# Two of three gate projections by Strassen's scheme on every second pair of weight rows, and a merge that goes branch by branch

## The chip, the cores and the metric

The kernel runs on one core of a Trainium2 chip. The metric is the device time of one execution in microseconds (us), the median of several runs. A profiled execution of the same kernel gives the trace from which all rows below come.

## The reference, cut to what matters

One decoder layer over 256 tokens of 2048 channels: a combined input projection, three token mixers, a gated merge, an output projection and a layer norm, all in float32.

```python
u = x @ w_in[l]                                   # 256 x 2048 by 2048 x 16896
(a_q, ..., c_g, m_a, m_b, m_c) = jnp.split(u, split_idx, axis=-1)
y_a = (o_a * silu(a_g)) @ w_proj_hgrn[l]          # 256 x 1024 by 1024 x 2048
y_b = (o_b * silu(b_g)) @ w_proj_attn[l]
y_c = (o_c * silu(c_g)) @ w_proj_conv[l]
merged = sigmoid(m_a) * y_a + sigmoid(m_b) * y_b + sigmoid(m_c) * y_c
x = layer_norm(ALPHA * x + merged @ w_out[l], ln_g[l], ln_b[l])
```

The change concerns `m_b` and `m_c`, the gate projections of the second and third branch: each is a product of 256 x 2048 by 2048 x 2048.

## The kernel before

A float32 product is made of three matmuls in a rounded format (float32r). Each operand is split into a part `hi` (the value rounded) and a part `lo` (the rest), and hi*hi + lo*hi + hi*lo is accumulated in PSUM. `x` is split once, into the tiles `xs`. The weights are split as they stream in: `load_granule` issues a DMA of 1 MB into one of three buffers `raw` (on SP's queue), and `split_w` makes of each half of it `hi` (a cast on ACT, L111) and `lo` (a subtraction on DVE, L112). `hi` and `lo` have four buffers each, of 128 x 1024.

`gemm` accumulates one block of 512 output columns for both halves of the tokens in two of the four PSUM banks `acc`. In the form "rows" (L140 to L142) one half granule serves two k-tiles (128 rows of weights each), two token halves and three matmuls, so 12 matmuls of 128x512.

The merge is the loop over four blocks `d` of 512 columns, and in it over the three branches: the gate (`rows512`, 16 k-tiles), its sigmoid (L637, on ACT), the projection of the branch (8 k-tiles), and on DVE the product with the gate and the sum (L641, L642, L644). `turn` transposes a finished block `merged` on TensorE (tiles `mT`, L259) and splits it into a tile `m`, the stationary operand of the output projection `w_out`. It is a task: `pump` lets it take one step after each half granule.

Around that stage: the conv mixer (`conv`, four calls) ends the mixers, and splits its result `yc` into the tiles `outs["c"]` (`oc`). In the merge all of this goes through a scheduler, which sets the order of instructions on each engine when the kernel is built; each engine then works through its own list in that order.

Of the kernel before, what the change touches and what calls it, by code (L numbers as in the profile page):

```python
# [36 lines left out]
HALF = 1024  # L37
# [11 lines left out]
def hybrid_kernel(ctx, tc, a, out):  # L49
    nc = tc.nc  # L50
# [22 lines left out]
    def bank(name):  # L73
        return bgp.tile([P, NC], F32, tag="bg", name=name)

    def f32(ap):
        return ap.bitcast(F32)


    xs = [t8([P, 4, 2, T], f"xs{i}", F32R) for i in range(4)]  # L80

    def split_to(dst, src):

        nc.scalar.copy(out=dst[:, :, 0], in_=src)
        nc.vector.tensor_sub(out=dst[:, :, 1], in0=src, in1=f32(dst[:, :, 0]))
# [7 lines left out]
    tasks = []  # L93
# [41 lines left out]
    def accumulators():  # L135
        return [accp.tile([P, NC], F32, tag="acc", name="acc") for _ in range(2)]
# [419 lines left out]
    ps = bank("warm")  # L556
# [4 lines left out]
    for hf in range(2):  # L561
        v = rows_out(rows512(AI + hf, None if hf else first), "va")
        q = t4([P, 4, T], "qa")
        for u in range(2):
            acc = columns256(AQ + 2 * hf + u)
# [7 lines left out]
        for u in range(2):  # L573
# [15 lines left out]
    acc = columns256(BK)  # L589
# [9 lines left out]
    for hf in range(2):  # L599
        gate = t4([P, 4, T], "gb")  # L600
        for u in range(2):
            acc = columns256(BG + 2 * hf + u)
# [5 lines left out]
        for u in range(2):  # L608
            acc = columns256(BQ + 2 * hf + u)
# [20 lines left out]
    branches = ((MA, "w_proj_hgrn", "a"), (MB, "w_proj_attn", "b"), (MC, "w_proj_conv", "c"))  # L630
    for d in range(4):
        m = t4([P, 2, NC], "merged")
        for n, (mc, wp, br) in enumerate(branches):
            acc = rows512(mc + d)
            sg = t4([P, 2, NC], "sg")
            for t in range(2):
                nc.scalar.activation(out=sg[:, t], in_=acc[t], func=AF.Sigmoid)  # L637
            acc = gemm(a[wp][d], outs[br], NC, "rows")
            for t in range(2):
                if n:  # L640
                    nc.vector.tensor_mul(out=sg[:, t], in0=acc[t], in1=sg[:, t])  # L641
                    nc.vector.tensor_add(out=m[:, t], in0=m[:, t], in1=sg[:, t])  # L642
                else:
                    nc.vector.tensor_mul(out=m[:, t], in0=acc[t], in1=sg[:, t])  # L644
        tasks.append(turn(m))
# [41 lines left out]
    for n in range(3):  # L687
        acc = gemm(a["w_out"][n], ms, NC, "rows")
# [3 lines left out]
    for g in range(4):  # L692
        raw = load_granule(a["w_out"][3, g])
# [18 lines left out]
def _weights(w, n):  # L712

    k, m = w.shape
    per = 2 * HALF // n
    return np.ascontiguousarray(
        w.reshape(k // (P * per), per, P, m // n, n).transpose(3, 0, 2, 1, 4)
    ).reshape(m // n, k // (P * per), P, 2 * HALF)


def _w_in(w):

    segment = lambda at, width: w[:, at : at + width]
# [75 lines left out]
```

## Time and profile before

| what | value |
|---|---|
| median of 3 runs | 1021.34 us (1020.45 to 1021.34) |
| the profiled execution | 1020.65 us, of it 1018.9 us span from the first to the last instruction |
| busy share of the span | TensorE 99%, its weight loads 83%, DVE 65%, ACT 51%, GpSimd 3% |
| granted TensorE clock | 0.996 of full speed |

The span is the stretch of the trace, and the time of the execution has 1.75 us more. A matmul's end is modelled and matmuls overlap, so the busy share says only that TensorE was hardly ever without one; its pace is read from the distance between starts.

### The profile page before, as it was taken

Reading aid. Unit: us, or ns where it says so; the run is one execution under the profiler, and the core shown is the slowest. Engines: PE = TensorE matmul, PEld = TensorE weight load, DVE = VectorE, ACT = ScalarE, POOL = GpSimd, SP = SyncE. Lnnn points to the kernel's source line nnn. Section 1 sums busy time; section 2 is a strip of 40 time slices with the busy share of each in tenths; the row PEclk is TensorE's granted clock in tenths of the full one; section 3 lists DMA queues with packets and bytes.
Section 4 is the critical chain, followed back from the end, with each engine's and each line's share of the span. In section 5 each row is a group of like instructions: output and inputs, shape, how many; then the busy total and the mean of one; then the engine's idle time right before and its main releaser. Section 6 shows DMA issues by size and latency. Waiting matters only on the chain.

```text
span 1018.9 us, 13636 instructions
## 1 busy us (share of the span) xinstructions
PE 1004.3 (99%) x5502; PEld 848.5 (83%) x5502; DVE 659.5 (65%) x828; ACT 516.9 (51%) x702; POOL 32.4 (3%) x32
## 2 busy tenths in 40 slices
PE   8999999999999999999999999999999999999995
PEld 5888888888888888888888888888888888888885
DVE  6557789689965777777764455445545455546666
ACT  5546577656564655656554434444444434444341
POOL 1000000300010000000000000000000000000003
PEclk9999999999999999999999999999999999999998
DMA  8654535353565445444455555555555546765442
GB/s 326 243 197 175 206 130 202 130 204 125 186 210 183 166 168 205 165 166 165 166 180 192 207 186 186 203 177 197 191 184 203 196 176 248 252 243 200 171 166 83
DMA packets 30255, 192.63 MB, mean 189 GB/s; under 512 B 3776, under 2 KB 4576, under 8 KB 8176
## 3 DMA queue, kind: packets, MB, share of 16 engines
q1 hardware_dynamic: 28368, 184.85, 51.1%
q10 hardware_dynamic: 1152, 4.72, 1.3%
q0 software_dynamic: 672, 2.20, 0.7%
q8 instruction: 43, 0.70, 0.3%
q14 instruction: 20, 0.16, 0.0%
HBM read 189.63 MB, written 2.12 MB: 188 GB/s over the span
## 4 chain that ended last, share of the span: by engine, by line
PE 94%; DVE 4%; DMA 1%; issue 0%; SPq 0%; ACT 0%
PE acc L148 23%; PE acc L142 19%; PE acc L140 19%; PE acc L141 19%; PE acc L147 11%; DVE lo L112 1%; PE sc L461 1%; DMA raw<-in_w_rows 1%; PE pvb L504 1%; PE acc L150 1%; PE pT L494 1%; PE pv L413 0%; PE mT L259 0%; PE lev L375 0%; PE lev L387 0%
## 5 line engine op out<-in xcount | busy, mean ns | idle before, releaser
L112 DVE TENSOR_TENSOR lo<-raw,hi 128x1024 fp32r<-128x1024 f32 (+1 forms) x341 | 414.9, 1220 | 289.4 <-ACT hi L111 288.3
L111 ACT CAST hi<-raw 128x1024 fp32r<-128x1024 f32 (+1 forms) x341 | 356.7, 1048 | 384.9 <-PE acc L141 264.4
L148 PE MATMUL acc<-xs,hi 128*128 128x512 f32 x1056 | 371.9, 396 | 0.0
L147 PE MATMUL acc<-xs,lo 128*128 128x256 f32 x990 | 278.5, 281 | 0.0
L148 PEld LDWEIGHTS acc<-xs,hi 128*128 128x128 f32 x1056 | 197.0, 188 | 43.7
L140 PE MATMUL acc<-hi,xs 128*128 128x512 f32 (+1 forms) x544 | 210.6, 387 | 1.3 <-ACT hi L111 1.3
L142 PE MATMUL acc<-lo,xs 128*128 128x512 f32 (+1 forms) x544 | 208.6, 384 | 0.8 <-DVE lo L112 0.8
L141 PE MATMUL acc<-hi,xs 128*128 128x512 f32 (+1 forms) x544 | 208.6, 383 | 0.0
L147 PEld LDWEIGHTS acc<-xs,lo 128*128 128x128 f32 x990 | 186.8, 189 | 2.3
L140 PEld LDWEIGHTS acc<-hi,xs 128*128 128x128 f32 x544 | 102.5, 188 | 23.9 <-ACT hi L111 3.8
L142 PEld LDWEIGHTS acc<-lo,xs 128*128 128x128 f32 x544 | 102.1, 188 | 22.4 <-DVE lo L112 2.3
L141 PEld LDWEIGHTS acc<-hi,xs 128*128 128x128 f32 x544 | 102.6, 189 | 19.6
L188 ACT COPY rest<-acc 128x256 f32<-128x256 f32 x66 | 24.3, 373 | 43.6 <-PE acc L148 42.8
L140 PE MATMUL acc<-hi,m 128*128 128x512 f32 (+1 forms) x120 | 45.2, 376 | 0.0
L142 PE MATMUL acc<-lo,m 128*128 128x512 f32 (+1 forms) x120 | 45.0, 375 | 0.0
L141 PE MATMUL acc<-hi,m 128*128 128x512 f32 (+1 forms) x120 | 45.0, 375 | 0.0
L141 PEld LDWEIGHTS acc<-hi,m 128*128 128x128 f32 x120 | 22.6, 188 | 4.0
L140 PEld LDWEIGHTS acc<-hi,m 128*128 128x128 f32 x120 | 22.6, 188 | 4.0
L142 PEld LDWEIGHTS acc<-lo,m 128*128 128x128 f32 x120 | 22.6, 188 | 4.0
L140 PE MATMUL acc<-hi,oa 128*128 128x512 f32 x64 | 24.9, 389 | 0.0
L141 PE MATMUL acc<-hi,oa 128*128 128x512 f32 x64 | 24.9, 389 | 0.0
L142 PE MATMUL acc<-lo,oa 128*128 128x512 f32 x64 | 24.9, 389 | 0.0
(187 smaller groups left out, 900.3 us busy)
## 6 DMA issues: line engine op xcount, KB each, us to landing
raw<-in_w_cols SPq DMA_DIRECT2D x68, 1024.0 KB, 4.8
raw<-in_w_rows SPq DMA_DIRECT2D x60, 1024.0 KB, 4.8
raw<-in_w_out SPq DMA_DIRECT2D x16, 1024.0 KB, 4.8
raw<-in_w_proj_hgrn SPq DMA_DIRECT2D x8, 1024.0 KB, 4.7
raw<-in_w_proj_attn SPq DMA_DIRECT2D x8, 1024.0 KB, 4.8
raw<-in_w_proj_conv SPq DMA_DIRECT2D x8, 1024.0 KB, 4.8
raw<-in_w_rows SPq DMA_DIRECT2D x7, 512.0 KB, 8.4
bias<-bias_dr POOLq DMA_DIRECT2D x2, 1024.0 KB, 6.1
```

The costliest lines, as they stand in the source:

```text
L111: nc.scalar.copy(out=hi, in_=r)
L112: nc.vector.tensor_sub(out=lo, in0=r, in1=f32(hi))
L140: nc.tensor.matmul(out=acc, lhsT=xk[:, 0, ts], rhs=hi, start=first, stop=False)
L141: nc.tensor.matmul(out=acc, lhsT=xk[:, 1, ts], rhs=hi, start=False, stop=False)
L142: nc.tensor.matmul(out=acc, lhsT=xk[:, 0, ts], rhs=lo, start=False, stop=last)
L147: nc.tensor.matmul(out=acc[:, :T], lhsT=lo, rhs=xk[:, 0], start=False, stop=False)
L148: nc.tensor.matmul(out=acc, lhsT=hi, rhs=xk, start=first, stop=last)
L150: nc.tensor.matmul(out=acc[:, :T], lhsT=lo, rhs=xk[:, 0], start=False, stop=False)
L188: nc.scalar.copy(out=rest[p], in_=acc[p, T:])
L461: nc.tensor.matmul(out=ps[:, o_ : o_ + 2 * nk], lhsT=q[:, 2 * g + x, m, blk * P : blk * P + P], rhs=kz[n][:, hf, :, 0:nk], start=(i == 0), ...
L494: nc.tensor.transpose(out=ps[:, x * P : x * P + P], in_=s[:, x // 2, x % 2, j * P : j * P + P], identity=C["ident"])
L504: nc.tensor.matmul(out=ps, lhsT=v[m][:, j, c], rhs=pT[n][:, j], start=(j == 0 and i == 0), stop=(j == blk and i == 2))
```

## The change

The gates of branches b and c are computed by `gate_pair`, one call for two blocks of 512 columns. The weights come in a layout of their own (`w_gate`): a granule of 1 MB holds a pair of k-tiles by 1024 columns, as four pieces of 128 x 512. A call goes through eight such pairs. Pairs 0, 2, 4 and 6 are done as before: 2 k-tiles by 2 column blocks by 2 token halves, 8 products of three matmuls each. Pairs 1, 3, 5 and 7 are done by a scheme of Strassen's kind with 7 products instead of 8. Its sums of weights are made on DVE (`w`, three instructions over 2048 columns in all) and split into `hw` (ACT) and `lw` (DVE); its sums of `x` are made once (`sums_of_x`). All products of a call accumulate in eight PSUM banks (`p1` to `p7` and `px`), four of them from the pool `bg` that the transposes use too. At the end one copy on ACT and eight sums on DVE make the two gates of the eight banks, and two sigmoids follow.

The merge goes branch by branch: branch a for all four blocks, then for b and for c two calls of `gate_pair`, each followed by the two projections of its blocks. The four blocks `merged` live through all of it. `oc` is split after the third call of `gate_pair` instead of in `conv`. The blocks are transposed in the last two projections and in `w_out`.

```diff
+PAIRS = (0, 1, 0, 1, 0, 1, 0, 1)
...
-        nc.vector.tensor_mul(out=y, in0=y, in1=h)
-        if u % 2 == 0:
-            outs["c"].append(t8([P, 4, 2, T], "oc", F32R))
-        split_to(outs["c"][-1][:, 2 * (u % 2) : 2 * (u % 2) + 2], y)
+        nc.vector.tensor_mul(out=yc[:, 2 * u : 2 * u + 2], in0=y, in1=h)
...
+    def sums_of_x():
+        n = len(pairs)
+        xr = rawp.tile([P, n, 2, T], F32, tag="raw", name="xr")
...
+        nc.vector.tensor_add(out=sx[:, 0], in0=x21, in1=x22)
+        nc.vector.tensor_sub(out=sx[:, 1], in0=sx[:, 0], in1=x11)
+        nc.vector.tensor_sub(out=sx[:, 2], in0=x21, in1=x11)
+        nc.vector.tensor_sub(out=sx[:, 3], in0=x12, in1=sx[:, 1])
+        yield
+        for i in range(0, n, 2):
+            dst = t8([P, 2, 4, 2, P], "sums", F32R)
+            sums.append(dst)
+            for j in range(2):
+                split_to(dst[:, j].rearrange("p s h t -> p s h t"), sx[:, :, i + j])
+            yield
...
+            w = t8([P, 4, NC], "w")
+            nc.vector.tensor_sub(out=w[:, 0:2], in0=raw[:, 0:1].to_broadcast([P, 2, NC]), in1=raw[:, 1::2])
+            nc.vector.tensor_sub(out=w[:, 2], in0=raw[:, 3], in1=w[:, 0])
+            nc.vector.tensor_sub(out=w[:, 3], in0=raw[:, 2], in1=w[:, 2])
+            hi, lo = split_w(flat[:, NC : 3 * NC])
...
+            split_w(flat[:, 3 * NC :], hi2, lo2)
...
+            split_w(w, hw, lw)
...
+            product(p1, block(k, 0), hi[:, :NC], lo[:, :NC], end)
+            product(p2, block(k + 1, 0), hi[:, NC:], lo[:, NC:], end)
+            pump()
+            product(p6, sx[1], hw[:, 2], lw[:, 2], end)
+            product(p7, sx[2], hw[:, 1], lw[:, 1], end)
+            product(p5, sx[0], hw[:, 0], lw[:, 0], end)
+            product(p3, sx[3], hi2, lo2, end)
+            product(p4, block(k + 1, 1), hw[:, 3], lw[:, 3], end)
+            pump()
...
+        nc.scalar.copy(out=one, in_=p1)
+        nc.vector.tensor_add(out=sg[0][:, 0], in0=p2, in1=one)
...
+        for y in sg:
+            nc.scalar.activation(out=y, in_=y, func=AF.Sigmoid)
...
+    for n, (wp, br) in enumerate((("w_proj_attn", "b"), ("w_proj_conv", "c"))):
+        for half in range(2):
+            sg = gate_pair(a["w_gate"][2 * n + half])
...
+            if br == "c" and half:
+                tasks.extend(turn(merged[d]) for d in range(2))
+            for j in range(2):
+                d = 2 * half + j
+                acc = gemm(a[wp][d], outs[br], NC, "rows")
...
+                if br == "c" and half:
+                    tasks.append(turn(merged[d]))
```

What the scheduler makes of it is shown at three places, as rows of an engine's list (line, operation, output <- inputs, size, and how often in a row).

First, DVE inside the merge. Before, in a block `d`:

```order
L112 TENSOR_TENSOR lo<-raw,hi 128x1024 x12
L641 TENSOR_TENSOR sg<-acc,sg 128x512 x2
L642 TENSOR_TENSOR merged<-merged,sg 128x512 x2
L112 TENSOR_TENSOR lo<-raw,hi 128x1024 x3
L85 TENSOR_TENSOR m<-mT,m 128x2x256
L112 TENSOR_TENSOR lo<-raw,hi 128x1024
L85 TENSOR_TENSOR m<-mT,m 128x2x256
```

Now, inside the second call of `gate_pair`, with buffer numbers; raw_6572 holds a direct pair, raw_6533 and raw_6606 the Strassen pairs before and behind it:

```order
L115 TENSOR_TENSOR lw_6548<-w_6535,hw_6547 128x2048
L115 TENSOR_TENSOR lo_6575<-raw_6572,hi_6574 128x1024
L691 TENSOR_TENSOR w_6608<-raw_6606 128x1024
L115 TENSOR_TENSOR lo_6591<-raw_6572,hi_6590 128x1024
L692 TENSOR_TENSOR w_6608<-raw_6606,w_6608 128x512
L115 TENSOR_TENSOR lo_6613<-raw_6606,hi_6612 128x1024
L693 TENSOR_TENSOR w_6608<-raw_6606,w_6608 128x512
L115 TENSOR_TENSOR lo_6617<-raw_6606,hi_6616 128x512
L115 TENSOR_TENSOR lw_6621<-w_6608,hw_6620 128x2048
```

Where one kind of instruction stood in long runs, DVE's list now repeats a group of eight for every two pairs, and `lw` stands two places behind the last sum `w` of its own pair.

Second, DVE at the end of the same call, where raw_6735 and those behind it hold the next projection:

```order
L115 TENSOR_TENSOR lo_6690<-raw_6679,hi_6689 128x512
L115 TENSOR_TENSOR lo_6738<-raw_6735,hi_6737 128x1024
L115 TENSOR_TENSOR lo_6754<-raw_6735,hi_6753 128x1024
L722 TENSOR_TENSOR sg_6718<-p2_6419,one_6721 128x512
L723 TENSOR_TENSOR u_6720<-p6_6420,one_6721 128x512
L115 TENSOR_TENSOR lo_6772<-raw_6769,hi_6771 128x1024
L724 TENSOR_TENSOR sg_6718<-p7_6421,u_6720 128x512
L725 TENSOR_TENSOR sg_6719<-p5_6422,u_6720 128x512
L726 TENSOR_TENSOR sg_6719<-p5_6422,sg_6718 128x512
L728 TENSOR_TENSOR sg_6719<-p3_6423,sg_6719 128x512
L727 TENSOR_TENSOR sg_6719<-p8_6425,sg_6719 128x512
L729 TENSOR_TENSOR sg_6718<-p4_6424,sg_6718 128x512
```

Three of the four halves of the projection's first block are split ahead of the last six sums. Before, the gates took nothing from DVE here (the first piece above).

Third, ACT around the start of `w_out`. Before, the last projection's sigmoids, then the first casts of `w_out` with the transposed last block `m` among them:

```order
L637 ACTIVATE sg<-acc 128x512
L111 CAST hi<-raw 128x1024
L637 ACTIVATE sg<-acc 128x512
L111 CAST hi<-raw 128x1024 x6
L84 CAST m<-mT 128x2x256
L111 CAST hi<-raw 128x1024
L84 CAST m<-mT 128x2x256
L111 CAST hi<-raw 128x1024 x16
```

Now, from the cast of the last half of the last projection on:

```order
L114 CAST hi<-raw 128x1024
L87 CAST m<-mT 128x2x256
L114 CAST hi<-raw 128x1024
L87 CAST m<-mT 128x2x256
L767 DMA xres_7858<-in_x 128x2048
L87 CAST m<-mT 128x2x256
L767 DMA xres_7859<-in_x 128x2048
L769 DMA lg<-in_ln_g 128x2048
L770 DMA lbt<-in_ln_b 128x2048
L87 CAST m<-mT 128x2x256
L114 CAST hi<-raw 128x1024
L87 CAST m<-mT 128x2x256
```

Only one half of `w_out` is cast ahead of the last block's two casts `m`, and the second half stands between them. On TensorE the eight transposes of that block follow directly behind the first 12 matmuls of `w_out`:

```order
L145 MATMUL acc<-lo,m 128x512
L262 MATMUL mT<-ident,merged 128x128 x8
L143 MATMUL acc<-hi,m 128x512
L144 MATMUL acc<-hi,m 128x512
L143 MATMUL acc<-hi,m 128x512
L144 MATMUL acc<-hi,m 128x512
L145 MATMUL acc<-lo,m 128x512 x2
```

Before, they came in two groups of four, behind the first 24 and the first 36 matmuls of `w_out`.

## Rows read from the trace of the kernel before

**Rows 1.** The page: busy time of the engines, and the chain that ended last.
```profile
PE 1004.3 (99%) x5502; PEld 848.5 (83%) x5502; DVE 659.5 (65%) x828; ACT 516.9 (51%) x702; POOL 32.4 (3%) x32
...
PE 94%; DVE 4%; DMA 1%; issue 0%; SPq 0%; ACT 0%
```

**Rows 2.** Stages: last mixers, whole merge, one block of it.
```profile
core 0: us, PE busy (x) PEld busy (x) DVE busy (x) ACT busy (x) POOL busy (x), PEclk, DMA share, GB/s
513.00:925.00 412.00, 412.00 (x1848) 341.66 (x1846) 216.19 (x204) 176.95 (x188) 0.00 (x0) 1.00 0.57 202
628.00:727.00 99.00, 99.00 (x443) 82.00 (x442) 51.52 (x48) 41.98 (x45) 0.00 (x0) 1.00 0.54 192
400.00:513.00 113.00, 112.98 (x646) 98.07 (x645) 85.41 (x130) 65.21 (x112) 0.00 (x0) 1.00 0.47 165
```

**Rows 3.** Waits in the merge: engine, line, waited for, us, times, longest.
```profile
ACT hi L111 <- PE acc L141: 213.8, 133, 2.2
DVE lo L112 <- ACT hi L111: 190.5, 138, 2.0
```

**Rows 4.** TensorE in order of time in a gate of the merge: start, us.
```profile
540.21 0.39 PE L140 MATMUL acc<-hi,xs 128*128 128x512 f32 x1
...
541.57 0.39 PE L140 MATMUL acc<-hi,xs 128*128 128x512 f32 x1
```

**Rows 5.** DVE in order of time where it never idled, in the mixers.
```profile
229.81 0.70 DVE L352 TENSOR_TENSOR PS<-PS 128x512 f32<-128x512 f32 x1
230.42 0.70 DVE L361 TENSOR_TENSOR e<-qc,el 128x512 f32<-128x512 f32 x1
231.02 0.70 DVE L353 TENSOR_TENSOR PS<-PS 128x512 f32<-128x512 f32 x1
231.62 1.23 DVE L112 TENSOR_TENSOR lo<-raw,hi 128x1024 fp32r<-128x1024 f32 x1
232.76 0.70 DVE L307 TENSOR_TENSOR nl<-e,nh 128x512 fp32r<-128x512 f32 x1
```

**Rows 6.** ACT in order of time where a gate ends.
```profile
545.85 0.60 ACT L637 ACTIVATE sg<-acc 128x512 f32<-128x512 f32 x1 [1.21 <-PE acc L142]
546.34 1.04 ACT L111 CAST hi<-raw 128x1024 fp32r<-128x1024 f32 x1
547.28 0.60 ACT L637 ACTIVATE sg<-acc 128x512 f32<-128x512 f32 x1
```

**Rows 7.** DVE in order of time behind a projection.
```profile
918.69 1.37 DVE L641 TENSOR_TENSOR sg<-acc,sg 128x512 f32<-128x512 f32 x2
919.97 1.29 DVE L642 TENSOR_TENSOR merged<-merged,sg 128x512 f32<-128x512 f32 x2
921.17 1.22 DVE L112 TENSOR_TENSOR lo<-raw,hi 128x1024 fp32r<-128x1024 f32 x1
```

**Rows 8.** DMA issues: median us from issue to landing, of 1 MB.
```profile
raw<-in_w_rows SPq DMA_DIRECT2D x60, 1024.0 KB, 4.8
```

**Rows 9.** The chain near the conv mixer's first call, in order of time.
```profile
249.26 0.60 DVE oc L85
...
251.69 1.24 DVE lo L112
252.97 0.38 PE acc L142
```

**Rows 10.** TensorE there: the wait in brackets.
```profile
252.97 0.38 PE L142 MATMUL acc<-lo,xs 128*128 128x256 f32 x1 [0.46 <-DVE lo L112]
```

**Rows 11.** TensorE at the start of `w_out`.
```profile
924.61 0.60 PE L259 MATMUL mT<-ident,merged 128*128 128x128 f32 x4
924.97 0.48 PE L140 MATMUL acc<-hi,m 128*128 128x512 f32 x1
```

**Rows 12.** ACT there.
```profile
924.58 1.05 ACT L111 CAST hi<-raw 128x1024 fp32r<-128x1024 f32 x1 [1.67 <-PE acc L141]
925.53 0.58 ACT L84 CAST m<-mT 128x512 fp32r<-128x512 f32 x1
```

More of the change, by code (lines that the diff above doesn't have):

```diff
@@ L40 @@
 POOL = 512
-AI, AG, MA, MB, MC = 0, 2, 4, 8, 12
+AI, AG, MA = 0, 2, 4
+PAIRS = (0, 1, 0, 1, 0, 1, 0, 1)
 AQ, AFG, BQ, BG, BK, BV = 0, 4, 8, 12, 16, 17
@@ L57, in hybrid_kernel @@
     w8 = ctx.enter_context(tc.tile_pool(name="w8", bufs=12))
-    w4 = ctx.enter_context(tc.tile_pool(name="w4", bufs=7))
     sm = ctx.enter_context(tc.tile_pool(name="sm", bufs=4))
+    mixers = ctx.enter_context(ExitStack())
+    w4 = mixers.enter_context(tc.tile_pool(name="w4", bufs=7))
     drp = ctx.enter_context(tc.tile_pool(name="drp", bufs=1, space=bass.MemoryType.DRAM))
@@ L579, in hybrid_kernel @@
         tasks.append(hgrn(hf, fk, q, v, gate))
+    yc = t8([P, 8, T], "yc")
     conv(0)
@@ L617, in hybrid_kernel @@
     pump(100)
+    mixers.close()
+    mgp = ctx.enter_context(tc.tile_pool(name="mgp", bufs=1, reuse_waits="tile"))
     ms = []
@@ L624, in turn @@
         ms.append(dst)
-        yield
         for i, ps in transpose_pairs([[m[:, t, c * P : c * P + P] for t in range(2)] for c in range(4)], "mT"):
@@ L628, in turn @@
             yield
-    branches = ((MA, "w_proj_hgrn", "a"), (MB, "w_proj_attn", "b"), (MC, "w_proj_conv", "c"))
-    for d in range(4):
[L632 to L645, printed above, removed]
+    pairs = [p for p in range(KT // 2) if PAIRS[p]]
@@ new lines, in hybrid_kernel @@
+    sums = []
+    def sums_of_x():
+        n = len(pairs)
+        xr = rawp.tile([P, n, 2, T], F32, tag="raw", name="xr")
+        for i, p in enumerate(pairs):
+            nc.sync.dma_start(out=xr[:, i], in_=a["xT"][:, 2 * p : 2 * p + 2])
+        x11, x21 = xr[:, :, 0, :P], xr[:, :, 0, P:]
+        x12, x22 = xr[:, :, 1, :P], xr[:, :, 1, P:]
+        sx = t8([P, 4, n, P], "sx")
+        nc.vector.tensor_add(out=sx[:, 0], in0=x21, in1=x22)
[9 more added lines that the diff above has]
+            yield
@@ new lines, in gate_pair, with product, block @@
+    def gate_pair(src):
+        p1, p2, p6, p7 = [accp.tile([P, NC], F32, tag="acc", name=f"p{i}") for i in (1, 2, 6, 7)]
+        p5, p3, p4, px = [bgp.tile([P, NC], F32, tag="bg", name=f"p{i}") for i in (5, 3, 4, 8)]
+        begun = set()
+        def product(ps, x, hi, lo, last):
+            begins = id(ps) not in begun
+            begun.add(id(ps))
+            nc.tensor.matmul(out=ps, lhsT=x[0], rhs=hi, start=begins, stop=False)
+            nc.tensor.matmul(out=ps, lhsT=x[1], rhs=hi, start=False, stop=False)
+            nc.tensor.matmul(out=ps, lhsT=x[0], rhs=lo, start=False, stop=last)
+        def block(k, t):
+            return [xs[k // 4][:, k % 4, i, t * P : t * P + P] for i in range(2)]
+        last = KT // 2 - 1
+        final = max(p for p in range(KT // 2) if not PAIRS[p])
+        for p in range(KT // 2):
+            raw = rawp.tile([P, 4, NC], F32, tag="raw", name="raw")
+            nc.sync.dma_start(out=raw, in_=src[p].rearrange("p (s n) -> p s n", s=4))
+            flat = raw.rearrange("p s n -> p (s n)")
+            if not PAIRS[p]:
+                for s in range(2):
+                    hi, lo = split_w(flat[:, s * HALF : s * HALF + HALF])
+                    k = 2 * p + s
+                    for c in (slice(0, NC), slice(NC, HALF)):
+                        second = (c.start == 0) == (s == 0)
+                        for t in (1, 0):
+                            ps = ((p2, p3), (p4, px))[t][second]
+                            product(ps, block(k, t), hi[:, c], lo[:, c], p == final and s == 1 and ps is px)
+                    pump()
+                continue
+            w = t8([P, 4, NC], "w")
[3 more added lines that the diff above has]
+            hi, lo = split_w(flat[:, NC : 3 * NC])
+            hi2 = hip.tile([P, HALF], F32R, tag="hi", name="hi")[:, :NC]
+            lo2 = lop.tile([P, HALF], F32R, tag="lo", name="lo")[:, :NC]
+            split_w(flat[:, 3 * NC :], hi2, lo2)
+            if pairs.index(p) % 2:
+                hw, lw = t8([P, 4, NC], "hw", F32R), t8([P, 4, NC], "lw", F32R)
+            else:
+                hw = mgp.tile([P, 4, NC], F32R, tag="hw", name="hw")
+                lw = mgp.tile([P, 4, NC], F32R, tag="lw", name="lw")
+            split_w(w, hw, lw)
+            i = pairs.index(p)
+            sx = [sums[i // 2][:, i % 2, j] for j in range(4)]
+            sx = [[y[:, 0], y[:, 1]] for y in sx]
+            k = 2 * p
+            end = p == last
+            product(p1, block(k, 0), hi[:, :NC], lo[:, :NC], end)
[6 more added lines that the diff above has]
+            product(p4, block(k + 1, 1), hw[:, 3], lw[:, 3], end)
+            pump()
+        sg = [mgp.tile([P, 2, NC], F32, tag="sg", name="sg", bufs=2) for _ in range(2)]
+        u = mgp.tile([P, NC], F32, tag="u", name="u")
+        one = mgp.tile([P, NC], F32, tag="one", name="one")
+        nc.scalar.copy(out=one, in_=p1)
+        nc.vector.tensor_add(out=sg[0][:, 0], in0=p2, in1=one)
+        nc.vector.tensor_add(out=u, in0=p6, in1=one)
+        nc.vector.tensor_add(out=sg[0][:, 1], in0=p7, in1=u)
+        nc.vector.tensor_add(out=sg[1][:, 0], in0=p5, in1=u)
+        nc.vector.tensor_add(out=sg[1][:, 1], in0=p5, in1=sg[0][:, 1])
+        nc.vector.tensor_add(out=sg[1][:, 1], in0=px, in1=sg[1][:, 1])
+        nc.vector.tensor_add(out=sg[1][:, 0], in0=p3, in1=sg[1][:, 0])
+        nc.vector.tensor_add(out=sg[0][:, 1], in0=p4, in1=sg[0][:, 1])
+        for y in sg:
+            nc.scalar.activation(out=y, in_=y, func=AF.Sigmoid)
+        return sg
@@ new lines, in hybrid_kernel @@
+    merged = [mgp.tile([P, 2, NC], F32, tag="merged", name="merged", bufs=4) for _ in range(4)]
+    tasks.append(sums_of_x())
+    for d in range(4):
+        acc = rows512(MA + d)
+        sg = mgp.tile([P, 2, NC], F32, tag="sg", name="sg", bufs=2)
+        for t in range(2):
+            nc.scalar.activation(out=sg[:, t], in_=acc[t], func=AF.Sigmoid)
+        acc = gemm(a["w_proj_hgrn"][d], outs["a"], NC, "rows")
+        for t in range(2):
+            nc.vector.tensor_mul(out=merged[d][:, t], in0=acc[t], in1=sg[:, t])
@@ new lines, in hybrid_kernel @@
+    pump(100)
+    for n, (wp, br) in enumerate((("w_proj_attn", "b"), ("w_proj_conv", "c"))):
+        for half in range(2):
+            sg = gate_pair(a["w_gate"][2 * n + half])
+            if br == "c" and not half:
+                for i in range(2):
+                    outs["c"].append(t8([P, 4, 2, T], "oc", F32R))
+                    split_to(outs["c"][i], yc[:, 4 * i : 4 * i + 4])
+            if br == "c" and half:
[3 more added lines that the diff above has]
+                acc = gemm(a[wp][d], outs[br], NC, "rows")
+                for t in range(2):
+                    nc.vector.tensor_mul(out=sg[j][:, t], in0=acc[t], in1=sg[j][:, t])
+                    nc.vector.tensor_add(out=merged[d][:, t], in0=merged[d][:, t], in1=sg[j][:, t])
+                if br == "c" and half:
+                    tasks.append(turn(merged[d]))
@@ L723, in _w_in, with _quads @@
     segment = lambda at, width: w[:, at : at + width]
-    in_rows = [segment(2048, HW), segment(3072, HW), segment(10752, 3 * D)]
+    in_rows = [segment(2048, HW), segment(3072, HW), segment(10752, D)]
     in_cols = [segment(0, HW), segment(1024, HW), _paired(segment(4096, HW)), _paired(segment(5632, HW)),
                segment(5120, 256), segment(5376, 256), segment(6656, 4 * HW)]
-    return (np.concatenate([_weights(x, NC) for x in in_rows]), np.concatenate([_weights(x, T) for x in in_cols]))
+    return (np.concatenate([_weights(x, NC) for x in in_rows]), np.concatenate([_weights(x, T) for x in in_cols]),
+            _quads(segment(10752 + D, 2 * D)))
+def _quads(w):
+    k, m = w.shape
+    blocks = w.reshape(k // (2 * P), 2, P, m // (2 * NC), 2, NC).transpose(3, 0, 1, 4, 2, 5)
+    order = [blocks[:, :, i, j] for i, j in ((0, 1), (0, 0), (1, 0), (1, 1))]
+    return np.ascontiguousarray(np.stack(order, 3)).reshape(m // (2 * NC), k // (2 * P), P, 4 * NC)
 def _paired(w):
@@ L767 @@
     x = np.ascontiguousarray(i["x"][0])
-    w_rows, w_cols = _w_in(i["w_in"][0])
+    w_rows, w_cols, w_gate = _w_in(i["w_in"][0])
     arrays = {
@@ L773 @@
         "w_cols": w_cols,
+        "w_gate": w_gate,
         "w_proj_hgrn": _weights(i["w_proj_hgrn"][0], NC),
```

## The prediction

> **What bounds the kernel now.** I read the page first: TensorE has a matmul in flight for 99% of the span and holds 94% of the chain that ended last, DVE 4% [rows 1]. Then the stages: in the merge, from 513 to 925 us, TensorE is never without work at full clock (1.00), DVE is busy 216.2 of 412 us and ACT 177.0 [rows 2]. The waits there show why: ACT waits for TensorE to give back a buffer `hi` (213.8 us in 133 waits), DVE waits for ACT (190.5 us) [rows 3]. Both run as far ahead as four buffers let them, four halves of 12 matmuls. So the merge takes as long as its matmuls, and their pace is six in 1.36 us, 0.2267 us each [rows 4].
>
> **The matmuls that go.** The two gates are 2 branches x 4 blocks x 16 k-tiles x 2 token halves x 3 = 768 matmuls of 128x512. Now there are four calls, each with four direct pairs of 24 and four Strassen pairs of 7 x 3 = 21: 720. The 48 that go are worth 48 x 0.2267 = 10.9 us, if TensorE stays fed. Projections, branch a and transposes keep their number.
>
> **What DVE has to do for it.** DVE instructions that follow each other start 0.60 us apart at 512 columns and 1.14 us at 1024 (231.62 to 232.76), although each lasts 0.70 and 1.23 us; the first passes its place on before it has ended [rows 5]. On ACT the distances are 0.49 and 0.94 us, at durations of 0.60 and 1.05 us [rows 6]. No row has 2048 columns: `lw` is bounded by one and two 1024-wide instructions, 1.14 and 2.28 us; by the step from 512 to 1024 I take 1.14 + 2 x 0.54 = 2.2 us. In the same way the cast `hw` takes 1.05 to 2.1 us, and I take 1.05 + 2 x 0.45 = 1.95. The sums `w`, one with a repeated operand, I take like other 512- and 1024-wide instructions; the bound above is the duration in place of the distance.
>
> DVE's list repeats every two pairs: three `lo` of 1024 (3.4), `w` (1.14 + 0.60 + 0.60), a `lo` of 512 (0.60) and `lw` (2.2), 8.6 us. And `lw` waits at the head of DVE's list: from the last `w` ACT needs 1.95 us for `hw`, in which DVE has only the short `lo`, so it stands for 1.35 us, with the next direct pair's `lo` behind it. That makes 9.9 us, against 45 matmuls x 0.2267 = 10.2 us on TensorE. DVE keeps pace, narrowly, and it begins a call with a lead.
>
> I followed the list of the second call with these distances, counted from the call's first matmul. Each buffer `hi` and `lo` comes free one period after its last use, so DVE may do a piece up to some 7 us before it is needed. The previous projection's products end at 1.2 and its sums at 2.4 (two products, two sums, then `lo`, 0.6 us apart [rows 7]). The first Strassen pair's `lo` is done at 3.8 and needed at 5.9; the second pair's `lw` at 14.5 and needed at 17.4; the third's at 24.6 and 27.6; the last's at 33.6 and 37.8. Slack 2 to 4 us each time: cost 0. What covers it is only that slack.
>
> The loads: three buffers, 4.8 us from issue to landing [rows 8]. The second Strassen pair's buffer is free at -2.9, so its weights land near 2 and are wanted at 5.6. Cost 0.
>
> **The end of a call.** Behind the last product stand a copy, eight sums (8 x 0.60 = 4.8 us) and two sigmoids. By the list three halves of the next projection are split ahead of the last six sums, 3 x 12 x 0.2267 = 8.2 us of matmuls. The sums end 3.3 us after the last product, the fourth half's `lo` at 4.4, needed at 8.6. The projection's banks are those of `p1` and `p2`, read before the call ends. Cost 0; without the three halves it would be some 4 us, four times. The split of `oc`, 2 x 1.14 us on DVE, now stands in front of this in the third call: the first `lo` behind it is done 3.3 us before TensorE is through. Cost 0.
>
> **The sums of x** are eight DVE instructions of 512 columns, 4.8 us, and 1 MB of load, in the last stretch of the mixers. DVE is busy 85.4 of 113 us there [rows 2]; with the lead of three halves, cost 0.
>
> **A small gain earlier.** Near 250 us DVE is on the chain, `oc` with 0.60 us in it [rows 9], and TensorE waits once, 0.46 us, for the `lo` behind it [rows 10]. That split is moved away: -0.5 (bounds 0 and -0.6).
>
> **The start of `w_out`.** Before, the last block was transposed behind 24 matmuls, with halves already split: four transposes and matmuls go on 0.36 us after the first [rows 11], a cast `hi` right before the cast `m` [rows 12]. Now one half only is split ahead. Counted from the last projection's end: its products and sums are done at 2.1; 12 matmuls of `w_out` end at 2.72; the first four transposes are done by 3.3 (0.60), all are issued by 3.45. ACT casts `m` from 3.35, and `hi` of the second half from 3.84 to 4.89. TensorE waits 1.45 us. Four matmuls with `hi` later, at 5.8, it wants `lo`, which DVE ends at 6.1: 0.3 us. Together +1.8 (bounds: 0, and 2.7 if the sums are late by 0.9).
>
> **Sum.** -10.9 - 0.5 + 1.8 = -9.6 us. On the profiled execution of 1020.65 us that is 1011.0; the median of the runs shown is 0.7 above it, so 1011.7.
>
> **Rivals.**
> *DVE is just too slow in the calls.* If each instruction holds its place for its whole duration, the group costs 3 x 1.23 + 1.23 + 3 x 0.70 + 2.3 = 9.3 us, and the wait for `hw` 1.25: 10.55 against 10.2. TensorE then loses up to 0.35 us in each of 16 periods, 5.6 us: 1017.3. For it: the margin is 0.3 us in 10.2, several of these instructions take turns with waits on other engines, and the rows of dense DVE work are from another stage. Against it: rows 5, the start of one instruction before the end of the other.
> The Trainium skill states this very rule (VectorE: DVE Perf Modes, "The DRAIN you can't avoid"): the next DVE instruction does not start until the pipe of the one before it is empty, so an instruction would cost its duration. By that the time is this rival's, 1017.3; the distances of 0.60 at durations of 0.70 in rows 5 speak against it.
>
> *Slower than before: the wait at the head of DVE's list reaches TensorE.* If DVE has no lead when a call starts, its 1.35 us behind `hw` fall on TensorE in each of 16 Strassen pairs: 21.6 us, 1033. It decides from 9.6 / 16 = 0.6 us per pair on. For it: `lw` has just two instructions between it and the sum it hangs on, and one list in order serves sums, splits and merge. Against it: two pairs of buffers for `hw` and `lw`, and needs that come 2 us and more after the results.
>
> *The work that goes is given back elsewhere.* The last call frees the four `bg` banks only with its last four sums, and the first transposes behind it want one of them. My list has the first bank free 1.2 us ahead of need. If DVE is 3 us late there, and the two waits at `w_out` grow to 2.7, and rival one holds as well, the gain is below 2 us. That the matmuls do not go is no rival: the list shows them gone.
>
> **How the numbers follow.** A measurement of this kernel tells about 0.2%, 2.0 us, from no change: 1019.3 to 1023.4 is "same". Forecast, 1009.9 (no wait at `w_out`, whole early gain) to 1014: 0.60. DVE somewhat too slow, 1014 to 1019.3: 0.22. Given back, same: 0.08. Slower: 0.10. So faster 0.82, same 0.08, slower 0.10. The range reaches to 1018.5, into the second case, and down to 1009.5.
>
> **What would show it.** Right: 48 matmuls fewer, at 0.227 us; in the four calls TensorE's waits for `lw` and `lo` near 0, DVE 85 to 90% busy (8.6 us of work in 10.2) with a wait of about 1.3 us before each `lw`; `lw` near 2.3 us long; one wait of 1.5 us for `hi` and a short one for `lo` behind the eight transposes. Wrong: waits of TensorE for `lw` in most pairs (rivals one and two, told apart by their size, 0.35 or over 1 us), or a lower granted clock behind such waits.

## The result, and the profile after

The changed kernel takes 1011.78 us (median of 4 runs, 1010.84 to 1012.6), the kernel before, measured beside it, 1021.23 us: a ratio of 0.9909, with a 95% interval of 0.9892 to 0.9926. The profiled execution took 1011.4 us, its span is 1009.6 us.

The page of after, busy times and the chain that ended last:

```profile
PE 993.0 (98%) x5454; PEld 839.3 (83%) x5454; DVE 743.5 (74%) x930; ACT 541.1 (54%) x716; POOL 32.4 (3%) x32
...
PE 97%; DVE 1%; DMA 1%; SPq 0%; ACT 0%; issue 0%
```

Against [rows 1], TensorE has 48 matmuls fewer, DVE 102 instructions and 84 us more, and yet DVE's part of the chain falls from 4% to 1%. Where the time went is read stage by stage. In the table of stretches, the merge runs from the first matmul of branch a's gate to the first of `w_out`, and the last stage from there to the end. First before, then after, where the row in the middle is the second call of `gate_pair` alone:

```profile
524.57:919.17 394.60, 394.60 (x1754) 326.77 (x1752) 204.71 (x191) 167.65 (x178) 0.00 (x0) 1.00 0.57 203
919.17:1018.90 99.73, 88.80 (x441) 75.33 (x439) 61.70 (x78) 36.45 (x42) 8.67 (x8) 0.96 0.42 152
```

```profile
524.26:907.98 383.72, 383.72 (x1706) 317.66 (x1704) 286.13 (x291) 190.81 (x190) 0.00 (x0) 1.00 0.58 203
717.38:758.18 40.80, 40.80 (x182) 33.78 (x180) 35.54 (x37) 21.87 (x21) 0.00 (x0) 1.00 0.58 203
907.98:1009.60 101.62, 89.29 (x441) 75.30 (x439) 64.05 (x80) 38.05 (x44) 8.67 (x8) 0.97 0.48 178
```

The merge is 10.88 us shorter, 48 x 0.2267, and TensorE has no wait in it that the table of waits lists. The last stage is 1.89 us longer. What lies ahead of 524 us is 0.31 us shorter. Together -9.30, the difference of the spans.

DVE in order of time within that call, from one `lw` to the next (start, duration, and in brackets the idle time before, with what ended it); it answers to the second piece of the list in the change and to [rows 5]:

```profile
729.46 2.29 DVE L115 TENSOR_TENSOR lw<-w,hw 128x2048 fp32r<-128x2048 f32 x1 [1.24 <-ACT hw L114]
731.68 1.23 DVE L115 TENSOR_TENSOR lo<-raw,hi 128x1024 fp32r<-128x1024 f32 x1
732.83 1.22 DVE L691 TENSOR_TENSOR w<-raw 128x1024 f32<-128x1024 f32 x1
734.13 1.22 DVE L115 TENSOR_TENSOR lo<-raw,hi 128x1024 fp32r<-128x1024 f32 x1
735.28 0.69 DVE L692 TENSOR_TENSOR w<-raw,w 128x512 f32<-128x512 f32 x1
735.88 1.22 DVE L115 TENSOR_TENSOR lo<-raw,hi 128x1024 fp32r<-128x1024 f32 x1
737.02 0.68 DVE L693 TENSOR_TENSOR w<-raw,w 128x512 f32<-128x512 f32 x1
737.73 0.69 DVE L115 TENSOR_TENSOR lo<-raw,hi 128x512 fp32r<-128x512 f32 x1
739.68 2.29 DVE L115 TENSOR_TENSOR lw<-w,hw 128x2048 fp32r<-128x2048 f32 x1 [1.26 <-ACT hw L114]
```

The period is 10.22 us, TensorE's own 10.2. The instruction behind `lw` starts 2.22 us after it, the one behind a 1024-wide `lo` 1.14 to 1.15, the one behind the first 512-wide `w` 0.60, each before the one ahead has ended, by 0.07 to 0.1 us. Behind the other two `w` it is 1.30 and 0.71 us, with a wait for `hi` too short for brackets. The Trainium skill (VectorE: DVE Perf Modes, "The DRAIN you can't avoid") says first that the next instruction does not start until the pipe is empty, and then, in the same paragraph, that one that is not held starts earlier. The prediction gave only the first half; the trace disagrees with that half taken alone, and is in line with the second. What holds an instruction back, no run here tests.

All `lw` of after, as the view of one tile gives them: durations (ns, min/median/max), and the idle time before them.

```profile
L115 DVE TENSOR_TENSOR lw<-w,hw x16: 2291/2292/2296, 652.3 to 873.8; 128x2048 fp32r<-128x2048 f32 x16
...
  ACT hw L114: 15.0, 16
```

DVE stands before each of the 16 for `hw`, 0.94 us on average; the view's list of who waited for `lw` is empty.

The one new wait is at the start of `w_out`. TensorE there, in order of time:

```profile
910.47 0.39 PE L145 MATMUL acc<-lo,m 128*128 128x512 f32 x1
910.70 1.03 PE L262 MATMUL mT<-ident,merged 128*128 128x128 f32 x8
912.92 0.50 PE L143 MATMUL acc<-hi,m 128*128 128x512 f32 x1 [1.18 <-ACT hi L114]
...
913.49 0.39 PE L143 MATMUL acc<-hi,m 128*128 128x512 f32 x1
913.72 0.40 PE L144 MATMUL acc<-hi,m 128*128 128x512 f32 x1
914.18 0.73 PE L145 MATMUL acc<-lo,m 128*128 128x512 f32 x2
```

And ACT:

```profile
911.34 0.59 ACT L87 CAST m<-mT 128x512 fp32r<-128x512 f32 x1 [8.06 <-PE mT L262]
911.82 1.05 ACT L114 CAST hi<-raw 128x1024 fp32r<-128x1024 f32 x1
```

The cast `hi` that TensorE wants stands behind a cast `m`, and ACT, with that `m` at the head of its list, was idle for 8.06 us until the transposes came. Before, a cast `hi` stood right before this `m` [rows 12], and the matmuls went on 0.36 us after the transposes [rows 11].

### The profile page after: what moved, and what is told of

Same layout as the page of the kernel before. It is cut to its first block, busy times and chain, and to the rows that moved or that the text cites. A ratio compares the mean times of both kernels' runs of the same rounds, so it can differ in the third digit from the quotient of the medians.

```text
span 1009.6 us, 13674 instructions
## 1 busy us (share of the span) xinstructions
PE 993.0 (98%) x5454; PEld 839.3 (83%) x5454; DVE 743.5 (74%) x930; ACT 541.1 (54%) x716; POOL 32.4 (3%) x32
## 4 chain that ended last, share of the span: by engine, by line
PE 97%; DVE 1%; DMA 1%; SPq 0%; ACT 0%; issue 0%
PE acc L151 24%; PE acc L145 13%; PE acc L143 13%; PE acc L144 13%; PE acc L150 12%; PE p L668 5%; PE p L667 5%; PE p L666 5%; DMA raw<-in_w_rows 1%; PE sc L464 1%; PE pvb L507 1%; PE acc L153 1%; PE pT L497 1%; PE lev L390 0%; PE pv L416 0%; PE lev L378 0%
## 5 line engine op out<-in xcount | busy, mean ns | idle before, releaser
L114 ACT CAST hi<-raw 128x1024 fp32r<-128x1024 f32 (+1 forms) x341 | 349.3, 1028 | 348.2 <-PE acc L144 143.4
L115 DVE TENSOR_TENSOR lo<-raw,hi 128x1024 fp32r<-128x1024 f32 (+1 forms) x341 | 404.5, 1194 | 175.0 <-ACT hi L114 173.4
L143 PE MATMUL acc<-hi,xs 128*128 128x512 f32 (+1 forms) x288 | 110.2, 383 | 2.3 <-ACT hi L114 2.3
L145 PE MATMUL acc<-lo,xs 128*128 128x512 f32 (+1 forms) x288 | 108.8, 379 | 0.4 <-DVE lo L115 0.3
L144 PE MATMUL acc<-hi,xs 128*128 128x512 f32 (+1 forms) x288 | 109.0, 378 | 0.0
L143 PEld LDWEIGHTS acc<-hi,xs 128*128 128x128 f32 x288 | 54.4, 189 | 14.8 <-ACT hi L114 4.4
L145 PEld LDWEIGHTS acc<-lo,xs 128*128 128x128 f32 x288 | 54.1, 188 | 11.5 <-DVE lo L115 1.6
L144 PEld LDWEIGHTS acc<-hi,xs 128*128 128x128 f32 x288 | 54.4, 189 | 9.8
L666 PE MATMUL p<-hi,xs 128*128 128x512 f32 x160 | 62.2, 389 | 0.0
L667 PE MATMUL p<-hi,xs 128*128 128x512 f32 x160 | 62.2, 389 | 0.0
L668 PE MATMUL p<-lo,xs 128*128 128x512 f32 x160 | 62.2, 389 | 0.0
L115 DVE TENSOR_TENSOR lw<-w,hw 128x2048 fp32r<-128x2048 f32 x16 | 36.7, 2293 | 15.0 <-ACT hw L114 15.0
L667 PEld LDWEIGHTS p<-hi,xs 128*128 128x128 f32 x160 | 30.0, 188 | 6.3
L666 PEld LDWEIGHTS p<-hi,xs 128*128 128x128 f32 x160 | 30.0, 188 | 6.2
```

The lines of the kernel that those rows point to most:

```text
L143: nc.tensor.matmul(out=acc, lhsT=xk[:, 0, ts], rhs=hi, start=first, stop=False)
L144: nc.tensor.matmul(out=acc, lhsT=xk[:, 1, ts], rhs=hi, start=False, stop=False)
L145: nc.tensor.matmul(out=acc, lhsT=xk[:, 0, ts], rhs=lo, start=False, stop=last)
L666: nc.tensor.matmul(out=ps, lhsT=x[0], rhs=hi, start=begins, stop=False)
L667: nc.tensor.matmul(out=ps, lhsT=x[1], rhs=hi, start=False, stop=False)
L668: nc.tensor.matmul(out=ps, lhsT=x[0], rhs=lo, start=False, stop=last)
```

## The experiments

My theory: the gain is the count of matmuls, 0.2267 us each, and stays whole because DVE's work of one period just fits under TensorE's; 1.8 us are given back at the start of `w_out`. The rivals: the gain comes from the order branch by branch, not from the scheme; DVE costs something already; the wait at `w_out` is not what it costs.

**No Strassen pairs.** All pairs direct; the order branch by branch stays.

```diff
-PAIRS = (0, 1, 0, 1, 0, 1, 0, 1)
+PAIRS = (0,) * 8
...
-        nc.scalar.copy(out=one, in_=p1)
...
+        for y, ps in ((sg[0][:, 0], p2), (sg[1][:, 0], p3), (sg[0][:, 1], p4), (sg[1][:, 1], px)):
+            nc.scalar.activation(out=y, in_=ps, func=AF.Sigmoid)
...
-    tasks.append(sums_of_x())
```

> No pair goes by the scheme: 768 matmuls in the gates as before, the merge still branch by branch, two column blocks of a gate per call, no sums of weights or of x, four sigmoids straight from PSUM. If the gain comes from the 48 matmuls: the time of before less the early 0.5 us, plus the wait of 1.3 to 1.8 us at the start of w_out, 1021.5 to 1023. If the gain comes from the new order of the merge or from oc being split later: near 1012.

Measured: 1022.3 us, ratio 1.0011 (1.0002 to 1.0021). Its merge (a row of the stretches) is as long as before, to the hundredth, and the wait of 1.18 us at the start of `w_out` is there too:

```profile
524.13:918.73 394.60, 394.60 (x1753) 326.67 (x1752) 203.06 (x189) 166.39 (x175) 0.00 (x0) 1.00 0.55 195
```

```profile
923.68 0.50 PE L143 MATMUL acc<-hi,m 128*128 128x512 f32 x1 [1.18 <-ACT hi L114]
```

So the reordering by itself brings nothing in the merge and costs at `w_out`; the whole gain of the merge is the scheme's.

**Half of the Strassen pairs.**

```diff
-PAIRS = (0, 1, 0, 1, 0, 1, 0, 1)
+PAIRS = (0, 0, 0, 1, 0, 0, 0, 1)
```

> Two of eight pairs by the scheme in each call (the fourth and the eighth) instead of four: 744 matmuls, half the sums. If TensorE is fed in every call and only the count of matmuls decides: 24 x 0.2267 = 5.4 us more than the changed kernel, 1017.2. If DVE is at its limit with four pairs and waits eat a part of what the matmuls give: less than 5.4 us more, 1012 to 1015.

Measured: 1016.33 us, ratio 0.9952 (0.9937 to 0.9966).

```profile
524.73:913.89 389.16, 389.16 (x1729) 322.16 (x1728) 253.66 (x254) 178.13 (x180) 0.00 (x0) 1.00 0.56 198
```

The merge lies 5.44 us below that without pairs, 24 x 0.2267, and 5.44 above after. The gain is in line with the matmuls that go, the theory's point. (By the medians it lies 4.55 above after, 0.9 less than forecast; the runs of the two kernels spread over 1.4 and 1.8 us.)

**One sum more on DVE.** The first sum `w` is made twice, 1.14 us more in each Strassen pair.

```diff
             nc.vector.tensor_sub(out=w[:, 0:2], in0=raw[:, 0:1].to_broadcast([P, 2, NC]), in1=raw[:, 1::2])
+            nc.vector.tensor_sub(out=w[:, 0:2], in0=raw[:, 0:1].to_broadcast([P, 2, NC]), in1=raw[:, 1::2])
```

> The first sum of each Strassen pair (128x1024) is made twice: 1.14 us more on DVE in each of 16 pairs, the output unchanged. DVE then needs 11.0 us where TensorE needs 10.2. If the slack of 2 to 4 us at the start of a call covers the first pairs: 0 to 8 us more than the changed kernel, likely 3 us. If DVE already is the limit of the calls: 16 x 1.14 = 18 us more, 1030. If DVE had much room: 0.

Measured: 1013.99 us, ratio 0.9931 (0.9916 to 0.9945); the merge is 386.17 us, 2.45 more than after, for 18.2 us of added work. Of the view of `lw`, the idle time before it and who waited for it:

```profile
  ACT hw L114: 10.6, 9
...
  PEld p L668: 1.8, 7
```

Now TensorE's weight loads do wait for `lw`, 7 times, 0.3 us at most. By the distance between first matmuls, the last three calls are 0.93 us longer together, and the first is not. The larger part, 1.52 us, lies in the projection behind the third call. DVE and TensorE there:

```profile
825.00 1.22 DVE L88 TENSOR_TENSOR oc<-yc,oc 128x1024 fp32r<-128x1024 f32 x1
```

```profile
827.40 0.74 PE L145 MATMUL acc<-lo,oc 128*128 128x512 f32 x2 [0.84 <-DVE lo L115]
```

The `lo` that TensorE waits for stands behind that `oc`. In after, three halves `lo` of this projection come ahead of the call's last six sums; here one does, and the others come behind all eight sums and both `oc`. So the calls themselves cover nearly all of the added work, and most of what it costs is the order that the scheduler writes.

**Three sums more on DVE.**

```diff
+            nc.vector.tensor_sub(out=w[:, 0:2], in0=raw[:, 0:1].to_broadcast([P, 2, NC]), in1=raw[:, 1::2])
+            nc.vector.tensor_sub(out=w[:, 0:2], in0=raw[:, 0:1].to_broadcast([P, 2, NC]), in1=raw[:, 1::2])
+            nc.vector.tensor_sub(out=w[:, 0:2], in0=raw[:, 0:1].to_broadcast([P, 2, NC]), in1=raw[:, 1::2])
```

> The first sum w is made four times over in each Strassen pair (three repeats, 3 x 1.14 = 3.4 us more of DVE per period; the result is the same). With one repeat the time rose by 2.4 us. Theory (a knee: DVE's group of 8.6 us and its wait before lw together just fill the 10.2 us of a period; what is added first eats the wait and the lead, then falls on TensorE in full): 12.0 us of DVE against 10.2, 1.8 us per pair and 29 us over 16 pairs, less up to 3 us of lead in each call: 1029 to 1041, with no wait left before lw. Rival (the cost is in line, as the first repeat's 2.4 us): 1019. Second rival (the wait before lw cannot be eaten): 3.4 - 0.3 = 3.1 per pair, 1055 to 1062.

Measured: 1038.65 us, ratio 1.0171 (1.0155 to 1.0186); the merge is 410.15 us, 26.4 more than after, where the first repeat had cost 2.45. The time lies in the theory's range, and the rise is not in line. But about 5 us of it are a lower clock (last section), which the theory did not have, and the waits (engine, line, waited for, us, times, longest) are not even shares of 1.8 us per pair:

```profile
PE p L666 <- ACT hw L114: 8.1, 4, 4.9
PE p L668 <- DVE lo L115: 6.4, 1, 6.4
```

The largest comes where the order of DVE's list has changed. Its rows ahead of that `lo`:

```profile
757.32 0.69 DVE L695 TENSOR_TENSOR w<-raw,w 128x512 f32<-128x512 f32 x1
757.92 1.23 DVE L694 TENSOR_TENSOR w<-raw 128x1024 f32<-128x1024 f32 x1
759.05 0.69 DVE L696 TENSOR_TENSOR w<-raw,w 128x512 f32<-128x512 f32 x1
759.65 0.69 DVE L695 TENSOR_TENSOR w<-raw,w 128x512 f32<-128x512 f32 x1
760.25 1.23 DVE L115 TENSOR_TENSOR lo<-raw,hi 128x1024 fp32r<-128x1024 f32 x1
```

L695 stands there twice: the sums of two pairs are interleaved, and a `lo` that TensorE wants at once stands behind both. So a DVE that is too slow does cost, but how much in one place is decided by the order that the scheduler writes. That also corrects the word "eaten" in the expectation: the wait before `lw` shrinks because other instructions have been placed in it.

**The four pairs in a row.**

```diff
-PAIRS = (0, 1, 0, 1, 0, 1, 0, 1)
+PAIRS = (0, 0, 0, 0, 1, 1, 1, 1)
```

> The same four Strassen pairs in a call, but as its last four in a row (pairs 4 to 7) instead of every second one. Matmuls stay at 720 for the gates, DVE's instructions too. Theory (what matters besides the count is that DVE's work of one period, and its lead, fit under TensorE's): a Strassen pair is 21 x 0.2267 = 4.8 us on TensorE, and on DVE w 2.3, lo 1.7 and lw 2.3, 6.3 us, with the wait for hw up to 7.6. Four in a row are 25 to 30 us of DVE against a lead of 5 to 7 and 14 to 16 us of matmuls ahead of the last lw: 3 to 10 us lost in each of four calls, 1023 to 1050 us, so the gain is gone, with waits of TensorE for lw in most pairs. Rival (only the count of matmuls decides): 1011.8, within 1.5.

Measured: 1015.87 us, ratio 0.9945 (0.9929 to 0.9962); the merge is 387.72 us, 4.0 more than after. The sign is the theory's, the size is neither's. TensorE at the end of the second call shows what I had left out:

```profile
756.99 0.39 PE L668 MATMUL p<-lo,sums 128*128 128x512 f32 x1
757.21 0.39 PE L143 MATMUL acc<-hi,ob 128*128 128x512 f32 x1
...
758.58 0.43 PE L666 MATMUL p<-hw,sums 128*128 128x512 f32 x1
...
760.94 0.87 PE L668 MATMUL p<-lw,sums 128*128 128x512 f32 x3
```

Matmuls of the next projection (`acc<-hi,ob`) stand inside the last Strassen pair, and `lw`'s own matmuls come last. The scheduler has moved the shortage behind other work; what is left are 2.0 us in 6 waits of weight loads for `lw`, and, in the projection behind the third call, where `oc` stands on DVE as well, a wait of 0.3 us for `oc` and one of 1.2 us for a `lo` behind it. The third call and its projection take 2.75 of the 4.0 us. The condition that DVE's work fits under TensorE's within the call was too narrow; it may also spill into the projection.

**The first sum on GpSimd.**

```diff
-            nc.vector.tensor_sub(out=w[:, 0:2], in0=raw[:, 0:1].to_broadcast([P, 2, NC]), in1=raw[:, 1::2])
+            nc.gpsimd.tensor_sub(out=w[:, 0:2], in0=raw[:, 0:1].to_broadcast([P, 2, NC]), in1=raw[:, 1::2])
```

> The first sum w (128x1024) is made on GpSimd instead of DVE, so DVE has 1.14 us less in each period. GpSimd takes 3.3 us for such an instruction in its one place in the mixers, so hw and lw come some 2 us later. Theory (DVE is below the knee, TensorE waits for nothing in the calls, and lw has 2 to 4 us of slack): no change, 1011.0 to 1012.5. Rival (DVE's margin costs something that shows as no wait, as in the first rival of the prediction): up to 5 us faster. Second rival (the late sum reaches TensorE, or GpSimd and DVE slow each other down): 16 x 1 us or more, 1020 and above.

Measured: 1017.44 us, ratio 0.9965 (0.9952 to 0.9978); the merge is 389.07 us, 5.35 more than after. So taking work off DVE made the kernel slower, as the second rival has it, though by far less than its figure. The timeline of all engines at the start of the second call, and TensorE's wait behind it:

```profile
721.86 2.53 POOL L691 TENSOR_TENSOR w<-raw 128x1024 f32<-128x1024 f32 x1 [9.87 <-DMA raw<-in_w_gate]
722.05 5.16 DVE L115 TENSOR_TENSOR lo<-raw,hi 128x1024 fp32r<-128x1024 f32 x3
```

```profile
725.53 0.50 PE L668 MATMUL p<-lo,xs 128*128 128x512 f32 x1 [0.97 <-DVE lo L115]
```

These three `lo` (the second has 512 columns) take 5.16 us; in after the same three take 2.96:

```profile
719.91 2.96 DVE L115 TENSOR_TENSOR lo<-raw,hi 128x1024 fp32r<-128x1024 f32 x3
```

All of the difference, 2.20 us, is in the first, which lasts 3.42 us in place of 1.22 and ends 1.08 us after GpSimd's sum. The same picture, a `lo` that starts just behind the start of GpSimd's sum, stands ahead of the waits of 0.97 us at 789.35 and 1.50 at 854.24. In the view of `lo` the longest lasts 3.43 us, the median 1.22:

```profile
L115 DVE TENSOR_TENSOR lo<-raw,hi x94: 678/1220/3432, 645.7 to 894.7; 128x1024 fp32r<-128x1024 f32 x78, 128x512 fp32r<-128x512 f32 x16
...
  PEld p L668: 5.4, 5
```

Of the 78 with 1024 columns, the five that start within a sum of GpSimd last 3.42 to 3.43 us, and none of the others over 1.23. The Trainium skill (SBUF — State Buffer, "Who interferes with whom") states that a DVE instruction with two inputs in SBUF contends with a GpSimd instruction that reads SBUF, and calls such contention an exclusive lock. The trace agrees: the first `lo` lost 2.20 us, where 2.34 us of GpSimd's sum were left, as far as GpSimd's rough times tell.

All five waits, 5.4 us of weight loads, are for `lo`, none for `lw`, and three of them, 4.7 us, end with a stretched `lo`. But the stretch alone hardly reaches TensorE: in after this `lo` is done 3.75 us into the call and first used at 5.89, 2.14 us to spare. The late sums do the rest. Counted from the call's first matmul, the last sum `w` of the pair, and with it `hw`, `lw` and what stands behind `lw`, comes 1.0 us later than in after, and `lo` starts 3.55 us into the call in place of 2.53. 1.02 + 2.20 - 2.14 is 1.08 us, near the 0.97 of the wait. GpSimd's sum itself takes 2.40 us (median of 16), not the 3.3 expected.

**The last block's transposes two steps later.** This is the version that the readings point to.

```diff
-    def turn(m):
+    def turn(m, late=0):
...
+        for _ in range(late):
+            yield
...
-                    tasks.append(turn(merged[d]))
+                    tasks.append(turn(merged[d], 2 * j))
```

> The task that transposes the last block waits two steps, so that ACT and DVE split a second half of w_out ahead of its casts and its lo. If the wait at the start of w_out is the one that I named (the cast hi of the second half behind the cast m): TensorE goes on behind the eight transposes at once, 1.3 us less, a span of 1008.3 and no wait there. If something else holds it (the sums of the last block): the wait stays.

Measured: 1009.96 us, ratio 0.9890 (0.9874 to 0.9907), 1.8 us below after. TensorE and ACT at the start of `w_out`:

```profile
910.94 1.03 PE L262 MATMUL mT<-ident,merged 128*128 128x128 f32 x8
911.73 0.48 PE L143 MATMUL acc<-hi,m 128*128 128x512 f32 x1
```

```profile
904.28 2.24 ACT L114 CAST hi<-raw 128x1024 fp32r<-128x1024 f32 x2 [0.77 <-DVE m L88]
911.58 0.59 ACT L87 CAST m<-mT 128x512 fp32r<-128x512 f32 x1 [5.05 <-PE mT L262]
```

TensorE's list has the transposes at the same place, but ACT's now has two casts `hi` ahead of the casts `m`, in the time in which it was idle. The matmuls go on 0.79 us after the transposes begin, not 2.22. From the first matmul of `w_out` to the end it takes 99.78 us, against 101.62 in after and 99.73 before. It is the fastest kernel here.

**The kernel before once more**, for its first 16 us.

> The kernel before, once more, for its first 16 us alone: the trace of after starts its fourth half granule 0.58 us later than that of before (TensorE waits 1.85 us for hi near 10.5 us, where it waited 0.68 and 0.66 us). If that is chance in the landing of the first loads, this trace shows a wait anywhere between 0.6 and 2.1 us in one place; if the change brought it, the two waits of 0.68 and 0.66 are there again. Time 1020.2 to 1022.

TensorE's longest wait there:

```profile
10.55 0.50 PE L140 MATMUL acc<-hi,xs 128*128 128x512 f32 x1 [1.84 <-ACT hi L111]
```

1020.73 us in this one execution. The wait of 1.84 us that I had seen in after alone is there without the change: it is chance in the first loads. The profiled execution of after has one wait more there (0.46 us), and so chance hides some tenths of the early gain.

## Why the prediction was right

It gave 1011.7 us; 1011.78 was measured. The terms, in its order:

**The matmuls that go**: -10.9 forecast, -10.88 measured in the merge, and shown to be the cause by the kernels with no pair (0) and with half of them (-5.44).

**DVE in the calls**: cost 0, as forecast. `lw` lasts 2.29 us and holds its place for 2.22 (taken: 2.2), `hw` lasts 1.91 (1.95), DVE is busy for 87% of the second call (85 to 90%). Counted from the call's first matmul at 717.38, the last three `lw` end at 14.4, 24.6 and 33.6 us and are first used at 17.5, 27.7 and 37.9; the forecast was 14.5, 24.6, 33.6 and 17.4, 27.6, 37.8. The wait before `lw` was put at 1.35 us; it is 1.24 and 1.26 in the middle of the call, less elsewhere. So the least slack of an `lw` is 3.1 us. The least of the call is that of the first Strassen pair's `lo`, done at 3.75 and first used at 5.89, 2.1 us (forecast 3.8 and 5.9). Pricing DVE's instructions by the distance of their starts gave these times to a tenth. The period came out longer than forecast: in the rows shown its eight instructions take 8.96 us from start to start and the wait 1.26, 10.22 us in place of 9.9. But the cast behind its longest wait for `hi` (0.09 us, at 734.13) had itself waited 1.4 us for TensorE to give back a buffer. In the middle of a call DVE thus goes at TensorE's pace, and how much room a period leaves is not to be read there.

**First rival, DVE just too slow**: false for this kernel. Whether its dearer prices alone would have cost time is not shown; the rival left out the lead. Its 0.35 us in each of a call's four periods are 1.4 us, less than the 2.1 us of least slack. One more instruction of 1.14 us per period brings the waits for `lw` that it describes, yet only 0.93 us in the calls; three bring 26 us, about 5 of them clock.

**Second rival, the wait at the head of the list**: DVE does wait, 15.0 us in sum, and none of it reaches TensorE.

**Loads, the end of a call, the sums of x, the split of `oc`**: cost 0; TensorE has no wait in the four calls or the projections behind them. The first `lo` behind `oc` ends 3.2 us before the third call does (forecast 3.3). That `oc` sits where little is to spare shows in the kernels with one more sum and with four pairs in a row, whose longest waits in the merge are there.

**The small early gain**: the wait of 0.46 us [rows 10] is gone, as forecast (-0.5). The same 500 matmuls around it, before and after, as rows of the stretches:

```profile
218.72:269.02 50.30, 49.84 (x501) 43.67 (x501) 48.97 (x78) 32.37 (x47) 2.37 (x3) 1.00 0.43 152
```

```profile
219.30:268.93 49.63, 49.63 (x501) 43.62 (x501) 48.45 (x77) 31.78 (x46) 1.47 (x2) 1.00 0.43 153
```

The second trace of before has 50.27 us here, the seven other kernels that split `oc` later 49.59 to 49.63. So 0.67 us are gained, a little over the bound of 0.6. What lies ahead of the merge as a whole is only 0.31 us shorter in the profiled execution: other stretches, that of the first loads among them, took about half of it back.

**The start of `w_out`**: +1.8 forecast, +1.89 measured. The transposes up to the next matmul take 2.22 us in place of the 0.79 of the version without the wait, 1.43 lost for `hi` (1.45); for `lo` 0.46 in place of 0.23 us, 0.23 lost (0.3); the other 0.2 us were not followed. Delaying the task gives 1.84 back, which shows it.

**Third rival, given back elsewhere**: nothing but `w_out` was.

So the mechanism was right, term by term. That the time fits to 0.08 us is in part luck: the runs of the changed kernel spread over 1.8 us, and the spans differ by 9.30 us where 9.6 was forecast.

What stays open: why single waits in the kernel with three repeats reach 6 us only where they do. The order of the list explains the largest; the others were not followed.

## What to carry to other kernels

Before trading matmuls for vector work, write down one period of each engine's list in distances between starts, with the wait at its head, and follow it against the times of need: here that gave the ends of `lw` to a tenth of a microsecond, and a least slack of 2 us that was there. Where a list is in order, look at what stands behind an instruction that must wait; a task delayed by two steps let idle ACT time do the next casts. And work moved from DVE to GpSimd is not free for DVE when both read SBUF at the same time: the same sum made the merge 5.35 us longer there.

## What the runs showed of the hardware

In the kernel with three repeated sums, TensorE comes back from its two longest waits at half its clock. The stretches behind the waits of 6.4 us (before 761.53) and 4.9 us (before 838.20), with the granted clock in the third column from the end:

```profile
740.00:754.00 14.00, 14.00 (x62) 11.32 (x62) 12.63 (x13) 5.62 (x6) 0.00 (x0) 1.00 0.55 204
761.50:766.00 4.50, 4.47 (x10) 3.20 (x11) 4.50 (x4) 4.43 (x5) 0.00 (x0) 0.50 0.59 224
...
838.20:844.00 5.80, 5.75 (x13) 4.07 (x14) 5.80 (x6) 1.84 (x2) 0.00 (x0) 0.50 0.81 335
```

0.50 is the lower of the two levels, 1.2 GHz: 4.5 and 5.8 us at half pace, so about 5 us of the 26.4 are clock and not wait. The waits of 1.2 us at the start of `w_out` brought no such fall: from the second matmul behind them on, the starts are 0.23 us apart again.
